# Summing the channel gate during the attention instead of ahead of the MLP

## The chip, the cores and the metric

The kernel runs on one core of a Trainium2 chip. The metric is the device time of one execution in microseconds (us). Every time and trace quoted here is of that one core. TensorE is called PE (PEld is its weight load), VectorE DVE, ScalarE ACT, GpSimd POOL and SyncE SP. SP issues all DMAs of this kernel.

## The reference

One layer of a streaming encoder on a sequence of 1024 tokens with 1024 channels, in float32:

```python
mod = silu(c) @ w_ada + b_ada                       # 6 rows of 1024
sh_a, sc_a, g_a, sh_m, sc_m, g_m = split(mod)
h = rmsnorm(x, g_attn_norm) * (1 + sc_a) + sh_a
proj = h @ w_in
o_mla = latent attention, 8 heads (low-rank q and kv, rotary part, chunk-causal)
o_ca  = chunked attention, 8 heads (9-chunk band, relative bias)
x = x + g_a * (concat(o_mla, o_ca) @ w_out)
h = rmsnorm(x, g_mlp_norm) * (1 + sc_m) + sh_m
u = causal depthwise convolution of width 3 over (h @ w_up)
gate, val = split(u)
x = x + g_m * ((silu(gate) * val) @ w_down)
```

`mod` has six rows of 1024 numbers, each a product of the vector silu(c) with a 1024x1024 block of `w_ada`. The change is about the last row, number 5, `g_m`: the gate of the channel sublayer. The other row that the text speaks of is number 2, `g_a`, and rows 3 and 4, shift and scale of the second norm.

## The kernel before

**Stages.** (1) Load `x`, norm it, compute rows 0 and 1, transpose `h` to channel layout and compute the first projection block. (2) The attention: 16 units of the chunked heads, then 16 units of the latent heads; a unit is 4 query tiles of one head. (3) Output projection of the latent heads, gated residual, second norm, transposes of the normed rows (`mod_transpose`, tile `ht_ps`). (4) The MLP: 44 column tiles of `w_up` (`up_tile`) and, in groups, `w_down` (`down`).

Matrix products are made in three products of split numbers (`gemm3`: high by high, high by low, low by high). So each weight tile is loaded raw, its high part is made by ACT (`hi_of`), its low part by POOL or DVE (`lo_of`).

**The attention and its fillers.** A query tile's steps are: scores on PE, softmax on DVE and ACT, a split into two half-precision parts (POOL, then DVE), a transpose by DMA (line 703, tile `PT`), and the product with V on PE (`pv`). Between these steps the code places other products, the fillers: the remaining projections (`qk1`, `qk2`, `v1`, `qk3`), the latent block (`m`), the up-projections of the latent heads (`up0`, `up1`) and the output projection of the chunked heads (`oca`). `pace` (called after every score and value step) runs fillers until an estimated PE cost is used up; `need` runs them until a named one is done. Each filler step says its own cost in ns of PE.

**The side work.** A generator `f_ada` (line 417) is advanced along the fillers. It makes rows 2, 3 and 4 in blocks of 256 columns: 8 loads of 128 KB of `w_ada` (`aw`, line 424) and a DVE multiply-add for each (`aacc`, lines 426 and 428), then a PE product that sums over partitions. For row 2 this is `gate_bcast` (line 449): it loads a piece of `b_ada` (`brow`), adds it, and multiplies with a matrix of ones, so that the sum stands on all 128 partitions; ACT copies it out (`gab`) and a DMA stores it to DRAM (`ga_d`). A block takes 6 steps of the generator. All these tiles come from `atile`, a pool of 3 buffers. `fill_step` (line 777) advances the generator by one step for each 2000 ns of filler cost, and not for `v0`, `up0`, `up1` and `oca`; what is left after the last filler is run at the end (`for _ in side[0]: pass`).

**Ahead of the MLP** (lines 892 to 908) row 5 is made in one piece: 8 loads of 512 KB into `adaw5`, summed by DVE (tile `adacc`, lines 902 and 904), `gate_bcast` twice with 512 columns (tile `p_gm`, line 454), and an ACT copy into `gmbc`. The `adaw5` tiles and the raw weight tiles of `up_tile` and `ff_tile` share one pool tag with 2 buffers:

```python
w = mp.tile([P, D], F32, name=f"adaw5_{k}", tag="raw", bufs=2)      # line 899
raw = mp.tile([P, ND, P], F32, name=f"wu_r{ch}", tag="raw", bufs=2) # line 911
```

`gmbc` is used when a raw tile of `w_down` is multiplied by it (line 938).

**What sets the order.** The order of instructions on each engine is fixed when the program is built: a list scheduler takes ready instructions by the order in the code, moved forward for the attention's steps (`high_priority`), on a model of the engines' times. Every engine, SP among them, then runs its list in order, and a tile is reused only after its last reader.

Of the kernel before, what the change touches and what calls it, by code (L numbers as in the profile page):

```python
# [12 lines left out]
F32 = mybir.dt.float32  # L13
# [4 lines left out]
AF = mybir.ActivationFunctionType  # L18
ALU = mybir.AluOpType
AX = mybir.AxisListType  # L20
PSUM = bass.MemoryType.PSUM
MUL, ADD, SUB, MIN, MAX = ALU.mult, ALU.add, ALU.subtract, ALU.min, ALU.max

P = 128
# [21 lines left out]

# columns of the packed constants
C_C, C_GA, C_GM, C_B, C_GQL, C_GKL = 0, 8, 16, 24, 72, 74
# [14 lines left out]
def layer_kernel(ctx, tc, I, out):  # L63
# [23 lines left out]
    part_d = dram.tile([NT, P, D], F32, name="part_d")  # L87
    ga_d = dram.tile([P, D], F32, name="ga_d")

    # ---------------- constants  # L90
    pk = cst.tile([P, NC_PACK], F32, name="pk")
# [23 lines left out]

    # =====================================================================
    # attention phase
    # =====================================================================
    right = tc.tile_pool(name="hw", bufs=1, side="right")
# [24 lines left out]
    def gemm3(pt, pairs, start=True, stop=True):  # L144
        """pairs: (stationary_hi, stationary_lo, moving_hi, moving_lo)"""
        n = len(pairs)
        for i, (sh, sl, mh, ml) in enumerate(pairs):
            pe.matmul(pt, sh, mh, start=(start and i == 0), stop=False)  # L148
            pe.matmul(pt, sh, ml, start=False, stop=False)  # L149
            pe.matmul(pt, sl, mh, start=False, stop=(stop and i == n - 1))  # L150

    # fillers: products that run between the steps of the attention, a few at a time,
    # queued behind the attention's latest products
    trail = []
# [11 lines left out]

    # ---- weights of one column block of the input projection, split once
    def load_w(name, src, ncol, he="a", ssw=None):
# [21 lines left out]

    # ---- x: statistics and normalised rows
    xs = []
# [20 lines left out]

    # ---- modulation rows and the first projection block, one slice of 128 channels at a time
    def mod_transpose(src, k, h, row, pspool, psum_tag, pb, hpool, tag, tmp, nbuf, veng, leng):
        """src(j): [128 tok, 128 ch] of 4 token tiles -> (hi, lo) of the modulated page [128, 2, 512]"""
        pt = pspool.tile([P, 512], F32, name=f"ht_ps{row}_{k}_{h}", tag=psum_tag, bufs=pb)
        for j in range(4):
            pe.transpose(pt[:, j * P:(j + 1) * P], src(j), ident[:])
        pg = hpool.tile([P, 2, 512], F32R, name=f"hT{row}_{k}_{h}", tag=tag, bufs=nbuf)  # L220
        a, b = modT[:, row, k:k + 1], modT[:, row + 1, k:k + 1]
        act.activation(pg[:, 0], pt[:], AF.Identity, scale=a, bias=b)
        v = tmp.tile([P, 512], F32, name=f"hv{row}_{k}_{h}", tag="hv", bufs=2)
        if veng == "a":
            act.activation(v[:], pt[:], AF.Identity, scale=a, bias=b)
        else:
            dve.tensor_scalar(v[:], pt[:], a, b, op0=MUL, op1=ADD)
        (dve if leng == "v" else pool).tensor_tensor(pg[:, 1], v[:], f32(pg[:, 0]), op=SUB)
        return pg
# [4 lines left out]
    for d in range(ND):  # L234
# [8 lines left out]
        for i in range(2):  # L243
            pe.matmul(pt[:, i:i + 1], acc[:, i, :], ones[:, 0:1], start=True, stop=True)
        # modT rows: 0 = gain of the norm * (1 + scale), 1 = shift
        tmp = cst.tile([P, 1], F32, name=f"adat{d}", tag="adat", bufs=2)
# [11 lines left out]

    # ---- rotary tables
    def rope_tables():  # L260
# [55 lines left out]
        act.activation(cn, cl2, AF.Sin)  # L316
        # per token: [g1 cos | g2 cos | g1 sin | g2 sin]
        for tab, c0 in ((tabq, C_RQ), (tabk, C_RK)):
# [11 lines left out]

    # ---- exact power-of-two scales that bring V into half precision's range, from a bound on |V|:
    # |sum_d x_d w_d|^2 <= n * sum_d b_d^2 w_d^2
    vscale = {}
# [25 lines left out]

    # ---- projection blocks  # L360
    def qk_norm(src_psum, nm, qn, j0):
        """[128, 2 tok tiles x 256] in PSUM -> normalised rows"""
        raw = rtile(f"raw{nm}")
        act.activation(raw[:], src_psum, AF.Copy)
        sq = qtile(f"sq{nm}")
        act.activation(sq[:], raw[:], AF.Square)
        ss = cst.tile([P, 8], F32, name=f"ss{nm}", tag="ss", bufs=4)
        r = cst.tile([P, 8], F32, name=f"r{nm}", tag="rr", bufs=4)
        dve.tensor_reduce(ss[:], sq[:].rearrange("p (a b) -> p a b", a=8), axis=AX.X, op=ADD)
        rsqrt_mean(r[:], ss[:], HD)  # L370
        pool.tensor_tensor(qn[:, j0:j0 + 2, :].rearrange("p t (a b) -> p (t a) b", a=4),
                           raw[:].rearrange("p (a b) -> p a b", a=8),
                           r[:].unsqueeze(2).to_broadcast([P, 8, HD]), op=MUL)
# [41 lines left out]

    # ---- the other adaLN rows
    def f_ada():
        for m in (2, 3, 4):
            for n in range(4):
# [13 lines left out]
                pt = ps.tile([P, 512], F32, name=f"p_ada{m}_{n}", tag="mm", bufs=2)  # L433
                if m == 2:
                    gate_bcast(pt[:, :256], acc, c0, 256, atile)
                    g = atile(f"gab{n}")
                    act.activation(g[:], pt[:, :256], AF.Copy)
                    sp.dma_start(ga_d[:, n * 256:(n + 1) * 256], g[:])
                else:
# [9 lines left out]
    def gate_bcast(pt, acc, c0, w, alloc):  # L449
        """column sums of acc, and b_ada, on every partition"""  # L450
        br = alloc(f"brow{c0}")
# [3 lines left out]

    # ---- latent block
    latT = {}

    def rope_apply(o, x, tab, t, nh, tmp):
        """o, x: [128, nh, 32]; tmp: [128, 2*nh*32]"""  # L460
        a = tmp[:, 0:nh * 32].rearrange("p (a b) -> p a b", a=nh)
# [41 lines left out]

    # ---- q_up / kv_up of 4 heads: token-layout q, k (normalised, rotated) and V stacks
    G = {}
# [76 lines left out]

    # ---- output projection of the chunked heads, kept aside in DRAM
    def load_wo(k0, n, he, le):
# [25 lines left out]

    # ---- attention
    def qk_page(src, name, rows, tag, bufs, gain):
        """src(j) -> [128 tok, rows] token-layout AP for the 4 token tiles of a half"""
        pt = ps.tile([P, 512], F32, name=f"{name}_ps", tag="T", bufs=TB)
# [11 lines left out]
    class Unit:  # L626
        """4 query tiles of one head"""

# [5 lines left out]
        def scores(u, i):  # L634
            """scores of one query tile and their softmax, transposed in two half-precision parts"""
            qpg, kpgs = u.pages()
# [140 lines left out]
    def fill_step():  # L777
        while fillers:
            key, gen = fillers[0]
            try:  # L780
# [4 lines left out]
                continue  # L785
            if key not in ("v0", "up0", "up1", "oca"):
                nside[0] += c
                while nside[0] > 2000:
                    nside[0] -= 2000
                    next(side[0], None)  # L790
# [39 lines left out]

    # =====================================================================
    # output projection of the latent heads, gated residual, second norm
    # =====================================================================
    wo = [load_wo(0, n, "a", "v" if n else "p") for n in range(2)]
# [48 lines left out]

    # =====================================================================
    # gated MLP with a causal depthwise convolution
    # =====================================================================
    mlp = tc.tile_pool(name="mlp", bufs=1, side="right", reuse_waits="tile")
# [3 lines left out]

    # gate of the channel sub-layer, on every partition
    def mtile(name):
        return mp.tile([P, D], F32, name=name, tag="u", bufs=3)

    gmbc = mp.tile([P, D], F32, name="gmbc")
    acc = mtile("adacc5")
    for k in range(ND):
        w = mp.tile([P, D], F32, name=f"adaw5_{k}", tag="raw", bufs=2)
        sp.dma_start(w[:], I["w_ada"][k * P:(k + 1) * P, 5 * D:6 * D])  # L900
        if k == 0:
            dve.tensor_scalar(acc[:], w[:], cs[:, 0:1], None, op0=MUL)
        else:
            dve.scalar_tensor_tensor(acc[:], w[:], cs[:, k:k + 1], acc[:], op0=MUL, op1=ADD)
    pt = ps3.tile([P, 1024], F32, name="p_gm", tag="U", bufs=2)
    for h in range(2):
        gate_bcast(pt[:, h * 512:(h + 1) * 512], acc[:, h * 512:(h + 1) * 512], 5 * D + h * 512, 512, mtile)
    act.activation(gmbc[:], pt[:], AF.Copy)

# [61 lines left out]
def _inputs(a):  # L971
    """layouts only: every array keeps its type and values"""
    f = lambda n: np.ascontiguousarray(a[n][0])
# [63 lines left out]
```

## Time and profile before

| what | us |
|---|---|
| median of 3 executions | 1525.28 (1518.91 to 1527.24) |
| span of the profiled execution | 1526.0 |
| PE busy | 1338.1 (88%) |
| DVE busy | 824.4 (54%) |
| POOL busy | 664.7 (44%) |
| ACT busy | 487.4 (32%) |
| latter part of the attention (400 to 680), PE busy | 215.3 of 280 |
| second norm's end to the first MLP product (770 to 795), PE busy | 4.2 of 25 |
| MLP (820 to 1500), PE busy | 675.0 of 680 |

For the profiled execution the trace gives its span, from the first to the last instruction of the program; no separate time of it is listed. The span is 0.7 us above the median of the runs. "Busy" is the time in which an engine executes an instruction. A row of instructions gives the line of the kernel, the engine, the operation, the tiles written and read, and the count; the bracket behind a row is how long the engine idled before it and what ended that. Times in windows are microseconds from the span's start.

### The profile page before, as it was taken

How to read it: one execution, taken by the hardware profiler on the slowest of the kernel's cores; microseconds unless marked ns; L12 is line 12 of the kernel's file. 1: busy time of each engine (PE TensorE's matmuls, PEld its weight loads, DVE VectorE, ACT ScalarE, POOL GpSimd, SP SyncE). 2: the span in 40 equal slices, each digit the busy share in tenths (PEclk: the TensorE clock that was granted, in tenths of full speed). 3: DMA queues.
4: the chain of work that ended last, by engine and by line, in shares of the span. 5: the costliest groups of instructions: out<-in, count | busy, mean ns of one | idle time of the engine just before them, and what ended most of it. 6: DMA issues, size and time to landing. Idle time of an engine off the chain costs nothing.

```text
span 1526.0 us, 19445 instructions
## 1 busy us (share of the span) xinstructions
PE 1338.1 (88%) x7100; PEld 1111.0 (73%) x7100; DVE 824.4 (54%) x1536; ACT 487.4 (32%) x919; POOL 664.7 (44%) x720
## 2 busy tenths in 40 slices
PE   3859989998767888858739999999999999999997
PEld 2749878987646666646528888888888888888885
DVE  6864786566768768843742433344334343434343
ACT  5443353343545545532413211212122121221200
POOL 5264463473799735435725231514314142341510
PEclk9979978989878899977859999999999999999998
DMA  7323657463613678787142110202112020110202
GB/s 270 133 67 73 138 119 142 121 131 94 122 40 70 150 143 174 165 181 247 56 138 69 56 55 28 70 30 67 42 42 69 15 83 28 56 56 28 70 1 110
DMA packets 202460, 142.90 MB, mean 94 GB/s; under 512 B 146294, under 2 KB 181242, under 8 KB 201340
## 3 DMA queue, kind: packets, MB, share of 16 engines
q1 hardware_dynamic: 202364, 141.66, 36.0%
q8 instruction: 56, 0.92, 0.3%
q14 instruction: 40, 0.33, 0.1%
HBM read 93.90 MB, written 13.11 MB: 70 GB/s over the span
## 4 chain that ended last, share of the span: by engine, by line
PE 63%; DMA 14%; DVE 10%; POOL 7%; issue 3%; ACT 2%; SPq 1%; POOLq 0%; DVEq 0%; ACTq 0%
PE up L148 10%; PE up L149 10%; PE up L150 10%; DMA aw<-w_ada 6%; PE dn L148 5%; PE dn L149 5%; PE dn L150 5%; DMA PTm<-hlm 4%; PE sc L656 2%; DVE adacc L241 2%; DVE aacc L428 1%; PE sm L656 1%; PE pvc L714 1%; POOL hlm L71 1%; DMA adaw<-w_ada 1%
## 5 line engine op out<-in xcount | busy, mean ns | idle before, releaser
L148 PE MATMUL up<-hT,wu_h 128*128 128x512 f32 x704 | 275.1, 391 | 0.0
L149 PE MATMUL up<-hT,wu_h 128*128 128x512 f32 x704 | 274.3, 390 | 0.0
L150 PE MATMUL up<-hT,wu_l 128*128 128x512 f32 x704 | 274.1, 389 | 0.0
L951 DVE TENSOR_TENSOR x<-x,dn 128x1024 f32<-128x1024 f32 x88 | 107.4, 1220 | 179.8 <-PE dn L150 179.8
L924 DVE SCALAR_TENSOR_TENSOR u<-up,pk,u 128x1023 f32<-128x1023 f32 x44 | 56.4, 1283 | 232.1 <-ACT u L923 232.1
L923 ACT ACTIVATE u<-up,pk 128x1024 f32<-128x1024 f32 x44 | 53.1, 1208 | 386.0 <-PE up L150 386.0
L149 PEld LDWEIGHTS up<-hT,wu_h 128*128 128x128 f32 x704 | 132.4, 188 | 28.0 <-issue 0.5
L148 PEld LDWEIGHTS up<-hT,wu_h 128*128 128x128 f32 x704 | 132.4, 188 | 27.9 <-issue 0.5
L82 POOL TENSOR_TENSOR wu_l<-wu_r,wu_h 128x1024 fp32r<-128x1024 f32 x44 | 105.7, 2402 | 107.9 <-PE up L149 60.1
L150 PEld LDWEIGHTS up<-hT,wu_l 128*128 128x128 f32 x704 | 132.4, 188 | 27.7 <-POOL wu_l L82 0.2
L77 POOL TENSOR_SCALAR wd<-wd_r 128x1024 fp32r<-128x1024 f32 x22 | 23.1, 1050 | 290.2 <-PE dn L150 289.1
L148 PE MATMUL dn<-wd,g 128*128 128x512 f32 x352 | 138.0, 392 | 5.0 <-ACT g L75 5.0
L149 PE MATMUL dn<-wd,g 128*128 128x512 f32 x352 | 137.9, 392 | 0.0
L150 PE MATMUL dn<-wd,g 128*128 128x512 f32 x352 | 137.4, 391 | 0.0
L71 POOL TENSOR_SCALAR hlm<-Pm,rim 128x512 f16<-128x512 f32 (+4 forms) x88 | 62.8, 717 | 69.1 <-DMA PTm<-hlm 46.6
L75 ACT ACTIVATE wu_h<-wu_r 128x1024 fp32r<-128x1024 f32 x44 | 46.5, 1057 | 141.1 <-DMA wu_r<-w_up 141.1
L938 POOL TENSOR_TENSOR wd_r<-wd_r,gmbc 128x1024 f32<-128x1024 f32 x22 | 52.6, 2392 | 80.6 <-DMA wd_r<-w_down 80.6
L701 DVE SCALAR_TENSOR_TENSOR hlm<-Pm,rim,hlm 128x512 f16<-128x512 f32 (+4 forms) x88 | 70.2, 801 | 31.7 <-POOL hlm L71 31.4
L148 PEld LDWEIGHTS dn<-wd,g 128*128 128x128 f32 x352 | 66.6, 189 | 19.4 <-issue 5.4
L71 POOL TENSOR_SCALAR hlc<-Pc,ric 128x640 f16<-128x640 f32 (+2 forms) x64 | 45.9, 719 | 78.5 <-DVE ric L684 38.9
L656 PE MATMUL sm<-mk,mq 96*128 96x512 f32 (+3 forms) x288 | 70.0, 375 | 9.8 <-ACT Pm L681 9.0
L656 PE MATMUL sc<-k,q 64*128 64x512 f32 (+3 forms) x288 | 71.2, 376 | 7.4 <-ACT Pc L681 4.9
(276 smaller groups left out, 3031.8 us busy)
## 6 DMA issues: line engine op xcount, KB each, us to landing
wu_r<-w_up SPq DMA_DIRECT2D x44, 512.0 KB, 3.6
aw<-w_ada SPq DMA_DIRECT2D x96, 128.0 KB, 2.2
wd_r<-w_down SPq DMA_DIRECT2D x22, 512.0 KB, 3.5
x<-x SPq DMA_DIRECT2D x16, 512.0 KB, 9.3
adaw<-w_ada_a SPq DMA_DIRECT2D x8, 1024.0 KB, 4.8
wq_r<-w_qk SPq DMA_DIRECT2D x32, 128.0 KB, 2.6
wor<-w_out SPq DMA_DIRECT2D x16, 256.0 KB, 3.0
cl<-oT_d SPq DMA_DIRECT2D x16, 256.0 KB, 3.3
```

What stands on the lines that cost most here:

```text
L71: pool.tensor_scalar(o, i, s, 1.0, op0=MUL, op1=MUL)
L75: act.activation(o, i, AF.Copy)
L82: (pool if eng == "p" else dve).tensor_tensor(o, i, f32(hi), op=SUB)
L148: pe.matmul(pt, sh, mh, start=(start and i == 0), stop=False)
L149: pe.matmul(pt, sh, ml, start=False, stop=False)
L150: pe.matmul(pt, sl, mh, start=False, stop=(stop and i == n - 1))
L656: last = pe.matmul(s[:, c:c + w], qpg[rs_, a, q], kpgs[kh][rs_, b, ko:ko + w], start=(a == 0 and b == 0), stop=(a == 1))
L701: dve.scalar_tensor_tensor(hl[:, w:2 * w], pp, ri[:], hl[:, :w], op0=MUL, op1=SUB)
L923: act.activation(u[:], pt[:], AF.Identity, scale=pk[:, cv + 2:cv + 3], bias=pk[:, cv + 3:cv + 4])
L924: dve.scalar_tensor_tensor(u[:, 1:], pt[:, :S - 1], pk[:, cv + 1:cv + 2], u[:, 1:], op0=MUL, op1=ADD)
L938: pool.tensor_tensor(raw[:], raw[:], gmbc[:], op=MUL)
L951: dve.tensor_tensor(x1[t][:], x1[t][:], pt[:], op=ADD)
```

## The change

Row 5 becomes part of `f_ada`: it is made in four blocks of 256 columns like row 2, and stored to a new DRAM tile `gm_d`. Ahead of the MLP, the 8 loads, the sums, the products and the copy are gone; one DMA loads `gmbc` from `gm_d`. In `fill_step` the generator is advanced along all fillers but `v0`, and by one step per 1800 ns of filler cost in place of 2000. (The change also takes out comments and docstrings, which shifts line numbers; those lines are left out here.)

```diff
     ga_d = dram.tile([P, D], F32, name="ga_d")
+    gm_d = dram.tile([P, D], F32, name="gm_d")
...
     def f_ada():
-        for m in (2, 3, 4):
+        for m in (2, 3, 4, 5):
             for n in range(4):
                 acc = atile(f"aacc{m}_{n}")
...
-                if m == 2:
+                if m in (2, 5):
                     gate_bcast(pt[:, :256], acc, c0, 256, atile)
                     g = atile(f"gab{n}")
                     act.activation(g[:], pt[:, :256], AF.Copy)
-                    sp.dma_start(ga_d[:, n * 256:(n + 1) * 256], g[:])
+                    sp.dma_start((ga_d if m == 2 else gm_d)[:, n * 256:(n + 1) * 256], g[:])
...
-            if key not in ("v0", "up0", "up1", "oca"):
+            if key != "v0":
                 nside[0] += c
-                while nside[0] > 2000:
-                    nside[0] -= 2000
+                while nside[0] > 1800:
+                    nside[0] -= 1800
                     next(side[0], None)
...
-    def mtile(name):
-        return mp.tile([P, D], F32, name=name, tag="u", bufs=3)
-
     gmbc = mp.tile([P, D], F32, name="gmbc")
-    acc = mtile("adacc5")
-    for k in range(ND):
-        w = mp.tile([P, D], F32, name=f"adaw5_{k}", tag="raw", bufs=2)
-        sp.dma_start(w[:], I["w_ada"][k * P:(k + 1) * P, 5 * D:6 * D])
-        if k == 0:
-            dve.tensor_scalar(acc[:], w[:], cs[:, 0:1], None, op0=MUL)
-        else:
-            dve.scalar_tensor_tensor(acc[:], w[:], cs[:, k:k + 1], acc[:], op0=MUL, op1=ADD)
-    pt = ps3.tile([P, 1024], F32, name="p_gm", tag="U", bufs=2)
-    for h in range(2):
-        gate_bcast(pt[:, h * 512:(h + 1) * 512], acc[:, h * 512:(h + 1) * 512], 5 * D + h * 512, 512, mtile)
-    act.activation(gmbc[:], pt[:], AF.Copy)
+    sp.dma_start(gmbc[:], gm_d[:])
```

## The prediction

> **What bounds the kernel now.** I read four views, in this order: busy time by stretches, the order of time around the end of the attention, the waits (of the engines, then of the DMA queue), and the rows of the loads that the change multiplies. The columns of the first are the stretch, its length, busy time and instruction count of PE, PEld, DVE, ACT and POOL, the granted clock, the DMA share and GB/s.
>
> ```profile
> 300.00:350.00 50.00, 47.64 (x294) 41.07 (x295) 34.31 (x104) 21.71 (x72) 35.79 (x62) 0.90 0.60 128
> 350.00:400.00 50.00, 42.15 (x250) 35.19 (x248) 32.13 (x87) 20.43 (x61) 23.06 (x49) 0.87 0.52 112
> 400.00:450.00 50.00, 32.09 (x151) 24.97 (x150) 35.18 (x93) 24.14 (x63) 45.96 (x87) 0.77 0.27 61
> 450.00:510.00 60.00, 48.69 (x278) 39.29 (x278) 49.71 (x131) 37.35 (x87) 57.10 (x100) 0.82 0.41 85
> 590.00:680.00 90.00, 68.22 (x501) 54.10 (x501) 65.02 (x158) 40.56 (x86) 40.49 (x50) 0.93 0.78 162
> 770.00:795.00 25.00, 4.21 (x6) 1.90 (x7) 11.76 (x11) 1.89 (x2) 2.63 (x2) 0.50 0.55 168
> 820.00:1500.00 680.00, 674.98 (x2974) 558.56 (x2974) 273.73 (x209) 135.24 (x125) 212.55 (x101) 1.00 0.15 47
> ```
>
> From 820 to 1500 PE is busy 675 of 680 us: the MLP is PE's own work, and whatever lets it start earlier ends the kernel earlier by as much. Directly before it PE works 4.2 us of 25. The attention has no such single limit: up to 400 PE nearly fills it (89.8 of 100 us), from 400 to 510 it is POOL (103 of 110), and after that no engine passes 76%.
>
> ```profile
> 766.09 1.97 PE L219 MATMUL ht_ps<-ident,xn 128*128 128x128 f32 x8 [0.93 <-DVE hv L227]
> 771.51 13.44 SPq L900 DMA_DIRECT2D adaw<-w_ada  x6
> 788.74 1.28 DVE L904 SCALAR_TENSOR_TENSOR adacc<-adaw,cs,adacc 128x1024 f32<-128x1024 f32 x1 [1.50 <-DMA adaw<-w_ada]
> 790.79 3.78 PE L454 MATMUL p_gm<-adacc,ones 128*128 128x512 f32 x4 [22.74 <-DVE adacc L453]
> 791.41 1.06 ACT L75 ACTIVATE wu_h<-wu_r 128x1024 fp32r<-128x1024 f32 x1 [22.55 <-DMA wu_r<-w_up]
> 793.59 1.42 PE L148 MATMUL up<-hT,wu_h 128*128 128x512 f32 x1
> 796.47 0.40 PE L150 MATMUL up<-hT,wu_l 128*128 128x512 f32 x1
> ```
>
> Here the hole is seen whole: the last transposes end at 768.06, the first `up` product starts at 793.59, 25.5 us later. Two waits hold it open together: `p_gm` stands ahead of `up` on PE, and the first `wu_r` could not be loaded, since its two `raw` buffers were taken by the eight `adaw` loads.
>
> ```profile
> SPq L424 <- DMA aw<-w_ada: 45.4, 34, 2.9
> SPq L438 <- ACT gab L437: 11.2, 2, 9.8
> PE pvm L714 <- DMA PTm<-hlm: 25.6, 21, 4.0
> L424 SPq DMA_DIRECT2D aw<-w_ada x96: 327/346/1147, 57.6 to 419.4; - x96
> L428 DVE SCALAR_TENSOR_TENSOR aacc<-aw,cs,aacc x84: 416/484/1544, 66.6 to 421.6; 128x256 f32<-128x256 f32 x84
> 294.19 0.49 POOL L113 TENSOR_SCALAR ss<-ss 128x8 f32<-128x8 f32 x1 [5.14 <-DVE ss L369]
> 286.01 0.20 POOL L113 TENSOR_SCALAR ss<-ss 128x8 f32<-128x8 f32 x1 [3.73 <-DVE ss L369]
> ```
>
> What the added work costs where such work already stands: SP holds 45.4 us for the slot of a load (waits by engine, count, longest), once 9.8 us for a `gab`; the values of the attention wait for transposes that go through the same SP. The loads end at 419; none stand in the latent heads.
>
> **The change, part by part.**
>
> *Removed, ahead of the MLP.* Eight 512 KB loads, eight DVE sums, two `brow`, four `p_gm` products and the copy into `gmbc`. What replaces the 25.5 us is the next thing that is late. The first `adaw` was issued at 746.29, when the last product of the output projection (745.8) freed the region. I take the same moment for what now comes first: `gmbc`, then `wu_r` twice, on SP. A 512 KB `adaw` landed after 4.4 us, so three behind one another land by about 746.3+3×4.4=759.5, the first `wu_r` by 755. ACT needs 1.06 us and POOL 2.36 us for it, in gaps that ACT shows at 1.3 and POOL at 1.6 us per pair of transposes: ready by about 761, before 768. The first 24 `up` products read pages of token half 0, done long before. So `up` can start at 768.06 or a little earlier between the transposes. Overshoot of POOL's gaps, 2.36−1.63=0.7 us for each of the first two tiles, delays the transposes by 0 to 1.5 us; `up` products slipped into PE's idle 5 us between 758 and 768 give back 0 to 2.3 us (ten products of 0.2275 us, the spacing at full clock). I set these against each other: 0.
>
> Clock: the stretch after the idle is granted 0.50, and `up` products take 0.63 us until 796.4, 0.39 after. Of that slow start of 5.6 us (790.8 to 796.4) `p_gm` now absorbs 2.8, `up` the rest. Without `p_gm` all of it falls on `up`: half of 2.8, 1.4 us more.
>
> So this part gains 25.5−1.4 = 24 us; bounds 19 (weights of the first tile ready only at 771.5 and a POOL delay) and 29 (a whole half tile, 24×0.2275=5.5 us, slipped in).
>
> *Added, in the attention.* Per block of 256 columns eight `aw` loads, a `brow`, a `gab` store; four blocks. SP: 32+4+4 issues at 0.346 us, 13.8 us. DVE: 28×0.484+4×0.354+4×0.406 = 16.6 us. PE: 4×0.377 = 1.5 us, ACT 4×0.381 = 1.5 us. Where: `f_ada` takes one step per 1800 of filler cost, from `qk1` on. The fillers `qk1`, `qk2`, `v1`, `qk3`, `m` sum to 120.2 us by their own formula, `up0` and `up1` to 13.0 each, `oca` to 41.4. Rows 2 to 4 have 72 steps, 130 us of filler; row 5 the next 24, up to 173 us. `m` ends at about 400 in the trace and `oca` runs from about 505 to 660, so row 5 stands between some 420 and 610, where the trace has none of these loads.
>
> Beside what: DVE has room (35 of 50, 50 of 60 us), SP too (at most 11.7 us of transposes in 20 us, 600 to 620). But the latent heads have no PE work in store, so delays show. Lower bound: nothing, since PE is idle 64 of the 280 us from 400 to 680 and the work fits the gaps. (Below nothing: a different order could also win a little; I know no reason that excludes some 3 us.) Upper bound: SP's queue in full. From the end of one DMA issue to the end of the next, a load took 1.36 us in the mean, a `gab` store 3.26, a `brow` 1.32: 32×1.36+4×3.26+4×1.32 = 62 us. Nearest row: 300 to 400 holds just 32 of these loads beside transposes, and PE is idle there 10.2 us (100−47.64−42.15) for any cause. Fillers covered part of the delays there, but not all of that idleness was the loads'. I take half, 5 us.
>
> POOL: its small `ss` takes 0.20 us, and 0.49 where it meets an `aacc`, 0.29 us more. With POOL the limit from 400 to 510, 28 such meetings would be 8 us, a third of them 2.7, which the 5 us include. [...]
>
> *Moved.* Rows 2 to 4 go at one step per 1800 in place of 2000: 66 steps in place of 60 by the end of `m`, in the part where PE is nearly full. The last two blocks, whose loads the trace already shows by 419 though the code has them at the end, get their products earlier than 662. Nothing waits for them before 736: 0. The reload of `gmbc` is counted above; its stores are done by 680.
>
> *Sum.* −24+5 = −19 us. The span is 1526.0; no time around it is given apart, and it stands 0.7 above the median of 1525.28. 1526.0−19 = 1507.0, against the median 1506.
>
> **The rivals.**
>
> *The added work costs nothing* and `up` slips in between the transposes: PE's 64 idle us and DVE's 30% speak for it, the values' 25.6 us of waiting for transposes against. 1525.3−24−0 to −29 = 1496 to 1501.
>
> *POOL or DVE pays in full.* Each `aacc` keeps POOL out for between the 0.29 us seen and its own 0.484: 28 of them 8 to 13.6 us, in 400 to 510; or DVE's 16.6 us stand in the path serially: 1525.3−24+8 to 16.6 = 1509 to 1518. For it: POOL 103 of 110. Against: row 5 reaches to 610, where POOL has half its time free.
>
> *SP blocks (slower).* SP runs in order; a load that waits for its buffer, or a `gab` store that waits for its product, holds back the transposes behind it, and PE waits for those. All 62 us on the path would end at 1563. It turns the sign at 24 of 62 us, 0.6 us per added issue on the path; slower by 0.5% needs 32, half of the queue time. For it: the 9.8 us `gab` wait, and DMA is 14% of the chain. Against: PE waited for the DMA of transposes 5.9 us in all from 300 to 400, with 32 loads there.
>
> *The hole does not close*: the weights' buffers come free late, or `gmbc` is late, so that little is won: 1518 to 1526. Against: their region is that of `adaw` and the freed output weights.
>
> **How the numbers follow.** Forecast (cost 2 to 8 us): 0.53. Nothing paid: 0.17. POOL or DVE: 0.14. SP blocks: 0.09. Hole stays: 0.07. The time is the first one's, 1506, with its own range 1502 to 1511. Down to 1496 and up to 1519 leaves out SP, the hole and some of the free case's tail: 0.2. About 0.5% (7.6 us) is what a measurement here tells from no change. Faster: 0.53+0.17+0.13=0.83; same: 0.01 of POOL's and the hole, 0.08; slower: 0.09.
>
> **What would show it.** After: no `p_gm` wait; `up` starting within 3 us of the last transpose; `wu_r` issued near 746 on the old clock; `aw` loads up to 500 or 600 with SP waits L424 grown by less than 25 us; the last transposes of the second norm at most 8 us later than 768. Wrong: that end moved by 20 us or more, or PE waiting for `PTm` 25 us longer.

## The result and the profile after

The changed kernel takes 1529.55 us in the median of 12 runs (1526.94 to 1534.07); the kernel before took 1522.96 on the same chip (12 runs, 1518.42 to 1527.64). The ratio is 1.0053, with an interval of 1.0036 to 1.0069: the change makes the kernel about 0.5% slower. 1506 was forecast, and the measured time lies outside the range of 1496 to 1519. The profiled execution took 1529.33 us, with a span of 1527.5. The kernel before was traced in one of its longer executions (its span, 1526.0, is 3.0 us above the median of its 12 runs, while in all other traces of this text the span is 1.8 to 2.4 us below the execution's time), so its times in the trace are late by up to some 5 us against its median, an estimate from these figures.

The order of time around the start of the MLP, in the kernel after (start, length, engine, line, operation, tiles, count; the bracket is the idle time before and what ended it):

```profile
751.94 0.49 SPq L894 DMA_DIRECT2D gmbc<-gm_d  x1
752.48 20.78 SPq L898 DMA_DIRECT2D wu_r<-w_up  x2
788.25 1.97 PE L220 MATMUL ht_ps<-ident,xn 128*128 128x128 f32 x8 [0.93 <-DVE hv L228]
790.94 1.99 ACT L75 ACTIVATE wu_h<-wu_r 128x1024 fp32r<-128x1024 f32 x2
792.04 0.80 PE L149 MATMUL up<-hT,wu_h 128*128 128x512 f32 x1 [1.81 <-ACT wu_h L75]
795.27 0.80 PE L151 MATMUL up<-hT,wu_l 128*128 128x512 f32 x1 [1.07 <-POOL wu_l L82]
```

The hole is closed as the prediction said. The weights are asked for from 752 on (the second tile some 20 us later), no `p_gm` is there, and the first `up` product starts 1.8 us after the last transpose. But this transpose ends at 790.2 instead of 768.1. The first `up` product starts at 792.0, where before it started at 793.6: of 23.7 us taken out of the hole, 22.1 had been lost by then. (By the medians, which differ by 6.6 us, it is more: 6.6+23.7, less 2.8 us by which the MLP got longer, leaves 27.5 us, in keeping with the long execution that was traced before.)

Where they were lost is seen in the stretches of the kernel after (length, then busy time and count of PE, PEld, DVE, ACT and POOL, granted clock, DMA share, GB/s):

```profile
350.00:400.00 50.00, 45.66 (x241) 38.85 (x240) 29.83 (x86) 18.29 (x58) 20.32 (x46) 0.80 0.47 101
400.00:450.00 50.00, 36.28 (x171) 28.87 (x170) 38.38 (x102) 27.80 (x69) 42.07 (x80) 0.75 0.33 77
450.00:510.00 60.00, 41.81 (x237) 33.98 (x238) 49.47 (x120) 32.65 (x77) 56.75 (x99) 0.81 0.38 84
590.00:680.00 90.00, 74.80 (x502) 59.96 (x501) 67.62 (x166) 42.79 (x90) 39.33 (x48) 0.89 0.76 160
770.00:795.00 25.00, 12.33 (x44) 7.99 (x44) 18.67 (x21) 12.19 (x18) 16.92 (x14) 0.57 0.07 21
820.00:1500.00 680.00, 674.99 (x2979) 558.71 (x2977) 273.91 (x210) 135.45 (x126) 214.96 (x102) 1.00 0.15 47
```

The MLP is PE's own work as before. From 450 to 510 PE makes 237 products where it made 278; from 350 to 400 it makes 241 in 45.7 us where it made 250 in 42.2, at a clock of 0.80 instead of 0.87. The attention is behind by then and stays so: the chunked heads end 7.7 us later than before and the latent heads 23.5. Its busiest engines are the same, and no new one is full.

The waits of the whole span, of SP's queue and of PE, in the kernel after (waiter, what it waited for, us in all, times, longest). Line 439 is the store of a `gab`; its wait is put down to the ACT instruction that came last.

```profile
SPq L425 <- DMA aw<-w_ada: 38.5, 30, 4.0
SPq L439 <- ACT kraw L568: 12.6, 1, 12.6
PE pvm L715 <- DMA PTm<-hlm: 22.6, 14, 3.3
PE sm L657 <- ACT Pm L682: 18.6, 16, 6.4
```

The last of them in the kernel before:

```profile
PE sm L656 <- ACT Pm L681: 9.0, 11, 2.2
```

The loads in the kernel after:

```profile
L425 SPq DMA_DIRECT2D aw<-w_ada x128: 323/376/1570, 55.9 to 616.4; - x128
```

The 32 further loads stand up to 616, as forecast. SP's wait for their buffers did not grow (45.4 before, 38.5 now), nor did PE's wait for the transposed values (25.6 before, 22.6 now). A single new block of SP is seen: from 466 to 478.7 the store of a `gab` holds it for 12.6 us. One wait of PE did grow, that of the latent heads' scores (`sm`) for ACT, from 9.0 to 18.6; no rival had named it, and it does not explain the time by itself (in the kernels below it is 8.3 in the fast `e5`, but 7.1 in the slow `k2`). So none of the marks that the rivals named is large, and yet 22 us are gone. A trace of the whole change can't tell which part took them; the runs below take it apart.

### The profile page after: what moved, and what is told of

Same layout as the page of the kernel before. It is cut to its first block, busy times and chain, and to the rows that moved or that the text cites. A ratio compares the mean times of both kernels' runs of the same rounds, so it can differ in the third digit from the quotient of the medians.

```text
span 1527.5 us, 19553 instructions
## 1 busy us (share of the span) xinstructions
PE 1353.6 (89%) x7104; PEld 1125.6 (74%) x7104; DVE 832.3 (54%) x1562; ACT 489.2 (32%) x922; POOL 660.1 (43%) x720
## 4 chain that ended last, share of the span: by engine, by line
PE 54%; POOL 5%; DVE 4%; DMA 4%; issue 2%; ACT 2%; SPq 0%; POOLq 0%; ACTq 0%; DVEq 0%
PE up L151 11%; PE up L149 10%; PE up L150 10%; PE dn L149 5%; PE dn L150 5%; PE dn L151 5%; DMA PTm<-hlm 2%; PE sm L657 2%; PE pvm L715 1%; DVE hlm L702 1%; DMA cl<-oT_d 1%; DVE mm L676 1%; POOL hlm L71 1%; PE op L151 1%; POOL x L871 1%
## 5 line engine op out<-in xcount | busy, mean ns | idle before, releaser
L657 PE MATMUL sm<-mk,mq 96*128 96x512 f32 (+3 forms) x288 | 74.5, 393 | 19.1 <-ACT Pm L682 18.6
L429 DVE SCALAR_TENSOR_TENSOR aacc<-aw,cs,aacc 128x256 f32<-128x256 f32 x112 | 62.7, 560 | 43.8 <-DMA aw<-w_ada 42.9
```

Source lines behind the costliest of these rows:

```text
L657: last = pe.matmul(s[:, c:c + w], qpg[rs_, a, q], kpgs[kh][rs_, b, ko:ko + w], start=(a == 0 and b == 0), stop=(a == 1))
```

## The experiments

All ratios are against the kernel before on the same chip, with 95% intervals. In us, 0.1% is 1.5. The median of the kernel before lies between 1522 and 1524.6 from chip to chip, so ratios are compared, not medians. The milestones are from the profiled execution of each kernel.

### Row 5 and the pace, each alone

`e1`: the change, but with the pace of before. `e2`: the kernel before with the new pace only. `e3`: the change without row 5's work (row 5 is left out, and `gmbc` is loaded from row 2's store instead; so too in all kernels below that are said to be without row 5). `e5`: the kernel before without row 5's work.

```diff
 e1, in fill_step of the kernel after
-            if key != "v0":
+            if key not in ("v0", "up0", "up1", "oca"):
-                while nside[0] > 1800:        # and the line below
+                while nside[0] > 2000:
 e2, in fill_step of the kernel before: the reverse
 e3, in the kernel after
-        for m in (2, 3, 4, 5):
+        for m in (2, 3, 4):
-    sp.dma_start(gmbc[:], gm_d[:])
+    sp.dma_start(gmbc[:], ga_d[:])
 e5: e3 with e1's lines
```

> The changed kernel with the old pace: one step of the side work per 2000 ns of filler cost, and none along v0, up0, up1 and oca, so that row 5 stands at the end of the side work. Theory A (row 5's own loads, sums and stores cost the 22 us that the attention lost): the attention still loses them, 1520 to 1530 us. Theory B (the new pace, that is the new order of the instructions, costs them, whatever row 5 does): the attention ends as before and the hole is closed, 1499 to 1504. Both by halves: about 1512.

> The kernel before with nothing but the new pace (one step per 1800 ns, along all fillers but the first); row 5 is still made ahead of the MLP. Theory A: no change, 1521 to 1525 us. Theory B: the attention's 22 us are lost and the hole stays, 1543 to 1547. By halves: about 1533, since the scores of the chunked heads were already 7 to 10 us late in the changed kernel before the first load of row 5.

> The changed kernel without row 5: the side work makes rows 2 to 4 at the new pace, and the gate of the channel sublayer is loaded from row 2's store instead (row 5 is left out of the computation). Theory A: the hole is closed at no cost, 1499 to 1502 us. Theory B: the attention still ends 22 us late, 1521 to 1525. By halves: about 1511.

> The attention's side work as before (rows 2 to 4, one step per 2000 ns, not along v0, up0, up1, oca), row 5 left out of the computation (row 2's store is loaded in its place). It prices the hole alone. If the new pace cost the changed kernel 10 us and row 5's work 12 us, the attention ends here as before (first output-projection product at 685 to 688 us) and the time is 1524 less 24 to 28, 1496 to 1500. If any change in the code behind the attention moves the attention too, it ends some 10 us off, 1506 to 1510.

| kernel | median us | ratio | last value product, chunked heads | same, latent heads | last transpose | first `up` | span |
|---|---|---|---|---|---|---|---|
| before | 1522.96 | 1 | 411.6 | 681.3 | 768.1 | 793.6 | 1526.0 |
| after | 1529.55 | 1.0053 [1.0036, 1.0069] | 419.3 | 704.8 | 790.2 | 792.0 | 1527.5 |
| `e1` | 1549.64 | 1.0166 [1.0146, 1.0186] | 413.4 | 681.0 | 811.2 | 813.0 | 1548.4 |
| `e2` | 1541.49 | 1.0113 [1.0094, 1.0132] | 416.6 | 692.7 | 783.0 | 808.0 | 1539.3 |
| `e3` | 1522.20 | 0.9982 [0.9969, 0.9995] | 417.9 | 690.4 | 781.2 | 783.0 | 1517.8 |
| `e5` | 1502.12 | 0.9858 [0.9833, 0.9884] | 409.2 | 677.9 | 764.5 | 766.3 | 1501.9 |

The three parts come out of the table. Taking row 5 out and leaving all else gives −1.42%, 21.6 us: that is the hole (`e5`). The new pace costs 1.24%, 18.9 us, with no row 5 anywhere (`e3` against `e5`), and 1.13%, 17 us, with row 5 still ahead of the MLP and the hole still open (`e2`). Row 5's own work in the attention costs 0.71%, 10.8 us (after against `e3`; the two medians differ by 7.4). −21.6+18.9+10.8 = 8.1 us, the measured 0.53%; they add up by construction, since `e5` and `e3` are steps on the way from before to after.

`e1` shows why the pace was changed together with the rest. Without it row 5's steps are not used up by the fillers, and what is left is made in one piece behind the last of them, where PE has nothing else to do. PE's waits from 670 to 745 in `e1`:

```profile
PE p_ada L455 <- DVE aacc L454: 54.4, 4, 16.5
```

The hole was only moved there from the start of the MLP, and grew.

### The rate, or the fillers that count

The new pace has two halves: 1800 in place of 2000, and `up0`, `up1` and `oca` counted. `e6` and `e7` take one half each, without row 5; `g2` is the whole change but for the rate.

```diff
 in fill_step of e3
 e6: if key not in ("v0", "up0", "up1", "oca"):   with 1800
 e7: if key != "v0":                              with 2000
 g2: the kernel after                             with 2000
```

> As the run without row 5, with one step per 1800 ns but still not along up0, up1 and oca. If the denser steps in the chunked heads cost the 10 us: 1506 to 1510. If the steps along the latent heads' fillers cost them: 1496 to 1500. If it is each new order's own luck: anywhere between 1490 and 1520, with no sum of the two halves.

> As the run without row 5, with one step per 2000 ns, along all fillers but the first. If the denser steps cost the 10 us: 1496 to 1500. If the steps along the latent heads' fillers cost them: 1506 to 1510; the last two blocks of rows 2 to 4 are then the only work that has moved. If it is each order's own luck: anywhere between 1490 and 1520.

> The whole change, but with one step per 2000 ns as before, along all fillers but the first; row 5 in the attention. If the rate of 1800 cost 11 us there as it did without row 5 (1522.2 against 1511.1) and row 5's own work 7 us: 1516 to 1521, faster than the kernel before. If row 5's work costs more once the steps stand further apart and run to the end of the attention: 1525 to 1535.

| without row 5 | old fillers | all but `v0` |
|---|---|---|
| 2000 | `e5` 0.9858 [0.9833, 0.9884] | `e7` 0.9913 [0.9888, 0.9937] |
| 1800 | `e6` 1.0005 [0.9988, 1.0021] | `e3` 0.9982 [0.9969, 0.9995] |

`g2` took 1516.81 us, 0.9949 [0.9933, 0.9966]. So the rate is the larger half: 1.47% with the old fillers, 0.69% with all. Counting more fillers costs 0.55% at 2000 and costs nothing at 1800 (−0.23%). The halves don't add. Row 5's work costs 0.36% at 2000 (`g2` against `e7`), 5.5 us. With the rate left at 2000 the change would have made the kernel faster by 0.5%.

### Is it the density of the side work?

My theory then was that a step per 1800 is too dense: more loads and sums in the same stretch, with PE nearly full. It expects the time to fall steadily as the steps stand further apart. The rival: each rate is another order of all instructions, and the order decides. Four more rates, with the old fillers and no row 5, differ from `e6` in the number alone.

> The run without row 5 along the old fillers, with one step per 1900 ns: between 2000 (1502.1 us) and 1800 (1524.6 us). If denser steps cost by themselves, it lies between them, 1508 to 1518. Theory E, that each order meets or misses single stalls by chance: it may as well be at 1500 or at 1530.

> The run without row 5 along the old fillers, with one step per 2200 ns; 2000 gave 1502.1 us, 1900 1525.5, 1800 1524.6. If thinner steps are better by themselves: 1495 to 1502. If the rate of 2000 is a lucky order among many: 1510 to 1530.

> The run without row 5 along the old fillers, with one step per 2100 ns. So far the last value product of the attention ended at 677.9 us with 2000, 681.8 with 2200, 697.4 with 1900 and 693.5 with 1800. Theory F (steps denser than one per 2000 ns of filler cost cost 16 to 20 us, thinner ones nothing): that end at 677 to 683. Theory E (chance): anywhere from 672 to 700.

> The same with one step per 1950 ns, the smallest change from 2000. Theory F in its smooth form: the end of the last value product between that of 2000 and 1900, at 680 to 692 us. Theory E: anywhere from 672 to 700; an end beyond that of 1900 (697) or before that of 2000 (678) speaks for chance.

| ns per step | median us | ratio | last value product, latent heads | DVE's multiply-adds wait for loads, 100 to 700 |
|---|---|---|---|---|
| 1800 (`e6`) | 1524.56 | 1.0005 [0.9988, 1.0021] | 693.5 | 37.9 |
| 1900 (`g3`) | 1525.53 | 1.0023 [1.0005, 1.0041] | 697.4 | 41.7 |
| 1950 (`m2`) | 1519.12 | 0.9980 [0.9966, 0.9995] | 689.9 | 48.8 |
| 2000 (`e5`) | 1502.12 | 0.9858 [0.9833, 0.9884] | 677.9 | 41.2 |
| 2100 (`m1`) | 1522.98 | 0.9999 [0.9983, 1.0015] | 690.5 | 52.9 |
| 2200 (`g4`) | 1517.35 | 0.9967 [0.9953, 0.9981] | 681.8 | 46.0 |

The theory falls. 2000 is the fastest, with a slower kernel on both sides of it; 1900 is no faster than 1800, 1950 still loses most of it, and 2100 is as slow as 1800. At 2100 and 2200 a known wait is part of it: their last block is left over, and PE waits 11.6 and 11.0 us for its sums ahead of the output projection. Without it 2200 would stand near 1506, an estimate, so 2200 alone would not speak against the theory. But at 2100 the latent heads, too, end 12.6 us later than at 2000. The kernels that lose do so in different places. Those with 1800 that I followed (after, `e3`, `e6`) fall back between 178 and 193: PE idles 4.4, 4.1 and 4.0 us there, at a mean granted clock of 0.78, 0.89 and 0.77, where `e5` idles 1.4 us at 1.00. By these figures it is some 4 to 5 us of PE's work, an estimate. 1950 loses there too (4.4 us idle, 0.89); 1900 does not (1.3 us, 1.00), and falls back between 400 and 420 instead, where PE is busy 11.4 of 20 us and in `e5` 15.4.

How one such loss comes about can be seen in the trace. DVE in the kernel after, then PE:

```profile
184.92 0.49 DVE L429 SCALAR_TENSOR_TENSOR aacc<-aw,cs,aacc 128x256 f32<-128x256 f32 x1
185.44 0.75 DVE L624 SCALAR_TENSOR_TENSOR k<-k_ps,gk_ca,k 128x512 fp32r<-128x512 f32 x1
```

```profile
186.24 1.22 PE L657 MATMUL sc<-k,q 64*128 64x128 f32 x4 [3.81 <-DVE k L624]
```

The same two in the kernel before:

```profile
184.45 0.75 DVE L623 SCALAR_TENSOR_TENSOR k<-k_ps,gk_ca,k 128x512 fp32r<-128x512 f32 x1
```

```profile
185.25 0.72 PE L656 MATMUL sc<-k,q 64*128 64x128 f32 x4 [0.31 <-DVE k L623]
```

DVE runs its list in order, and waits for loads in it (of `aw`, 1.4 to 2.1 us each around here). In the kernel after, one sum more and an `oc` (the result of a value product) stand ahead of the split of `k` that PE's next scores need: `k` comes 1 us later. That alone would be little. But in the kernel before, PE had a value product and fillers ready for these 4 us, and in the kernel after it has almost none there. The stretches of after (columns as above), and then that of before:

```profile
182.00:186.00 4.00, 0.44 (x2) 0.24 (x2) 2.29 (x4) 0.00 (x0) 0.00 (x0) 1.00 0.22 66
186.00:189.00 3.00, 2.76 (x11) 2.53 (x12) 1.88 (x11) 1.02 (x4) 0.37 (x1) 0.54 0.21 44
189.00:192.00 3.00, 3.00 (x16) 3.00 (x15) 1.14 (x4) 1.23 (x2) 0.48 (x1) 0.50 0.15 30
192.00:196.00 4.00, 4.00 (x21) 2.87 (x20) 2.07 (x8) 0.67 (x2) 1.84 (x2) 0.87 0.25 60
```

```profile
182.00:186.00 4.00, 3.01 (x26) 2.54 (x25) 1.63 (x3) 0.69 (x2) 0.71 (x1) 1.00 0.40 104
```

The gap of 3.81 us is paid more than once: until about 193 PE then works at half the clock (0.54 and 0.50 from 186 to 192), so that it makes 27 products in 6 us. PE's busy time over the span grew from 1338.1 to 1353.6 us, with 7104 products in place of 7100; this place makes up some 3.4 us of it, an estimate (half of the time at half the clock), and the rest was not followed. In the kernel before, with its wait of 0.31 us, the granted clock is 1.00 from 182 to 196. After the gap of 3.81 us it took some 6.8 us to come back, from 186.24 to 193.0, worked out from the 0.87 of the last stretch. It is not always so long. In `e3` PE idles 3.50 us at the same place, and the stretch behind it is:

```profile
186.00:192.00 6.00, 6.00 (x33) 5.31 (x32) 3.23 (x12) 2.24 (x6) 1.54 (x4) 0.72 0.17 34
```

A mean of 0.72 over 6 us is 3.4 us at half the clock. In `e6`, with a gap of 3.45 us, the same stretch has 0.50, so it is 6 us or more there. The length of the gap alone does not decide it.

### The loads, or the sums

Since the pace moves loads (SP, DMA) and sums (DVE) alike, `h1` takes the loads away from `e6` (all sums read one resident tile) and `h2` the time of the sums (one column each). `i1` is the kernel after with one load for the eight sums of a row-5 block.

```diff
 h1, in f_ada of e6 (and atile's pool with 2 buffers, to make room for awc)
-                    w = atile(f"aw{m}_{n}_{k}")
-                    sp.dma_start(w[:], I["w_ada"][k * P:(k + 1) * P, c0:c0 + 256])
+                    w = awc
 h2, in place of the two sums of e6
+                    dve.tensor_scalar(acc[:, k:k + 1], w[:, 0:1], cs[:, k:k + 1], None, op0=MUL)   # and one memset of acc per block
 i1, around the load of the kernel after
+                    if m < 5 or k == 0:
```

> The 1800 run without row 5 and along the old fillers (1524.6 us, against 1502.1 at 2000), but all sums of the side work read one resident tile in place of 96 loaded ones (so rows 2 to 4 come out as other numbers; one of the side work's three buffers is given up for it). Theory C (at 1800 the sums stand in DVE's fixed order too early, wait there for their loads, and hold back the attention's own DVE work behind them): with nothing to wait for the loss goes, 1498 to 1508 us. Theory D (the sums' own DVE time, 51 us, is what costs): nothing goes, 1518 to 1525. Theory E (any new order of the instructions falls by chance): anywhere.

> The same 1800 run with the 96 loads, but each sum cut to one column, so that DVE waits for the load and then works next to nothing (rows 2 to 4 come out as other numbers). Theory C: the waits stay and most of the loss with them, 1515 to 1525 us. Theory D: the loss goes, 1495 to 1505. Theory E: anywhere.

> The changed kernel with one load in place of eight for each block of row 5, its eight sums all reading that tile (row 5 comes out as other numbers). If row 5's loads and their waits are what its 7 us in the attention are made of: 1521 to 1525 us, as without row 5 (1522.2). If its sums, products and stores are: 1527 to 1531, as the changed kernel (1529.6).

`h1` took 1496.91 us, 0.9819 [0.9802, 0.9836]; `h2` 1512.66, 0.9932 [0.9918, 0.9945]; `i1` 1522.82, 1.0004 [0.9993, 1.0016]. Without loads the rate of 1800 is faster than any kernel with loads: 28 us against `e6`, more than the pace costs. PE's wait for transposed values of the chunked heads between 140 and 420, first in `e6`, then in `h1`:

```profile
PE pvc L715 <- DMA PTc<-hlc: 9.2, 8, 2.9
```

```profile
PE pvc L717 <- DMA PTc<-hlc: 1.6, 3, 0.7
```

The chunked heads end at 390.2 in `h1` and at 416.1 in `e6`, so nearly all of it is won there. (The wait is 9.1 us in `e5` too: it is a price of the loads at either rate, not of 1800.) With the loads and nearly no sums, 11 us are won. In row 5's part, 28 of the 32 loads make 0.49% (after against `i1`), 7.5 us, most of row 5's 10.8. It is a mixed difference: from the end of the chunked heads to that of the latent heads `i1` needs 271.2 us and the kernel after 285.5, but its chunked heads end at 425.3, 6.0 us later than those of the kernel after, although in the kernel after all but two of row 5's loads stand behind that point. So the loads, waited for in queues that run in order, look like the larger part of what makes the side work dear, and the DVE time of the sums like the smaller. These runs change the order too, so each price has the scatter of the table of rates on it; and no kernel without loads was run at 2000, so how much of `h1`'s 28 us belongs to the rate of 1800 is not shown.

### Can the waiting be taken off DVE?

If a sum that waits for its load holds up what is behind it on DVE, loads issued a step earlier than their sums should help. `k1` is the kernel after with the two loads of a step issued ahead and their sums queued one step later, behind the latest split of the softmax (line 702); `k2` has the same sums in `v1`, the kernel told of next.

```diff
+                for k0 in range(0, ND, 2):
+                    ws = [load(k0), load(k0 + 1)]      # as before, two loads
+                    yield 0
+                    with (tc.issue_after(dtrail[-1]) if dtrail else ExitStack()):
+                        ...                            # their two sums
```

> The changed kernel, complete, with one thing more: the sums of a pair of loads are emitted one step later than the loads and queued on DVE behind the last split (line 702) that the attention has emitted by then. Theory C (sums that reach DVE's queue before their load has landed hold back the attention): DVE waits for the loads much less than the changed kernel's 43 us, and a large part of the 20 us lost in the attention comes back, 1505 to 1517 us. Theory E (any order loses by chance): waits fall but the time need not, 1510 to 1535.

> The best kernel so far (row 5 in the MLP with own buffers, the attention's side work as before, 1505.4 us) with the same late sums for rows 2 to 4. Theory C: part of the 41 us for which DVE waits for loads there goes, 1495 to 1503 us. Theory E: as likely slower as faster, 1497 to 1520.

DVE's wait for the loads from 100 to 700, in the kernel after and in `k1`:

```profile
DVE aacc L429 <- DMA aw<-w_ada: 40.7, 40, 2.8
```

```profile
DVE aacc L436 <- DMA aw<-w_ada: 33.3, 35, 3.8
```

The wait fell as meant (in `k2` to 25.7, from 38.9 in `v1`), and both became slower: `k1` 1541.85 us, 1.0117 [1.0094, 1.014], `k2` 1538.51, 1.0103 [1.009, 1.0117]. But this is no clean test of the idea. In `k2` the last sums, tied to the latest split, come only after the attention (the last load of `aw` at 721.0, in `v1` at 419.5), and PE waits for them ahead of the output projection, which it does not in `v1`. PE's wait from 680 to 800 in `k2`:

```profile
PE p_ada L445 <- DVE aacc L435: 25.3, 2, 16.5
```

These 25.3 us are most of the 33 us by which `k2` is slower than `v1`. In `k1` a load now holds SP once for 19.7 us and once for 12.1, waiting for its buffer in the latent heads; the longest such wait in the kernel after is 4.0:

```profile
SPq L428 <- DVE modT L451: 19.7, 1, 19.7
```

The chunked heads do end earlier with late sums, 9.9 us in `k1` and 5.1 in `k2`, and the loss lies behind them: from there to the end of the latent heads `k1` needs 305.8 us instead of 285.5, and `k2` 290.4 instead of 272.8. So these two runs show that late sums in this form don't pay, but not that DVE's waiting for loads costs nothing; that SP's new waits are the cause is not shown. In the table of rates, with the same work, the sum of DVE's waits does not rank the times: `e5`, the fastest, has more of it than `e6`. Where a wait falls seems to count for more than how much of it there is.

### Row 5 where PE covers it

The hole can also be closed with the attention left alone. `e4` and `v1` are the kernel before with row 5 behind the first two `up` tiles, so that PE has work while the row is loaded and summed. In `e4` the loads keep the two `raw` buffers that the weights use; in `v1` they and the sum stand in buffers of the MLP that are not needed yet (`g` and `wd`). Both put `p_gm` into PSUM tiles of `down`.

```diff
     def ff_tile(j):
         ug = up_tile(j)
         uv = up_tile(NF + j)
+        if j == 0:
+            gate_row()                       # the old block, as a function
 in gate_row, v1 against e4
-            w = mp.tile([P, D], F32, name=f"adaw5_{k}", tag="raw", bufs=2)
+        ws = [mp.tile([P, 2, S], F32, name=f"adaw5_{k}", tag="g", bufs=4) for k in range(2)]
+            w = ws[k // 2 % 2][:, k % 2]
```

> The kernel before, with row 5 made in one piece behind the first two column tiles of w_up instead of ahead of them, its products in the PSUM buffers of the down-projection; nothing in the attention is touched. Both theories: the attention ends as before, the hole at 770 closes, and row 5's sums lie beside PE's own work: before less 23 us, 1498 to 1502. If the hole has another cause than the loads and the place of the products of row 5, it stays at 1521 to 1525.

> Row 5 made in the MLP as in the run before with that place, but its loads and sums in buffers of the later g and wd tiles, so that the raw weight tiles wait for nothing. If that run's 25 us of PE idleness inside the MLP came from the raw buffers, they go: 1498 to 1503 us. If they came from the place of the gate's products in PE's order, ahead of weights that are ready, PE still waits for them, less long since four loads fly together: 1505 to 1515.

`e4` took 1534.55 us, 1.0066 [1.0043, 1.0088]. Its hole is closed (the first `up` at 765.9), but PE idles 29.9 us in the MLP where the kernel before has 5.0. PE's waits from 764 to 860, and SP's queue:

```profile
PE p_gm L454 <- DVE adacc L453: 18.7, 1, 18.7
```

```profile
769.14 37.10 SPq L898 DMA_DIRECT2D adaw<-w_ada  x8
```

The eight loads pass through the two `raw` buffers at the pace of DVE's sums, and no weights come in for those 37 us: the hole was moved again. With buffers of its own (`v1`) row 5 is loaded beside the weights, and PE idles 6.1 us in the MLP:

```profile
766.76 1.97 PE L219 MATMUL ht_ps<-ident,xn 128*128 128x128 f32 x8 [0.93 <-DVE hv L227]
770.54 0.79 PE L148 MATMUL up<-hT,wu_h 128*128 128x512 f32 x1 [1.81 <-ACT wu_h L75]
```

`v1` takes 1505.42 us (1501.77 to 1508.68), 0.9873 [0.985, 0.9896], with the whole computation. It beats both kernels, and stands 0.15%, 2.3 us, above `e5`, which has no row 5 at all; the intervals of the two overlap. Its attention ends as before (last transpose at 768.7).

## Why the prediction was wrong, step by step

**What bounds the kernel: right.** The MLP is PE's own work, and the 25.5 us ahead of it were open idle time. **Removed, −24: right.** `e5` gives 21.6 us and `v1` 19.3, both within the bounds of 19 to 29. The size was short by the two terms that I had set against each other: `up` did not start in the gaps of the transposes but 1.8 us after the last, since ACT makes `wu_h` only at 790.94, behind its last copy of the transposes, though the first weights had been asked for at 752.5. The time from the first `up` to the last `down` product grew by 2.8 us (727.5 to 730.3): PE's busy time in it by 1.8, where the clock had been taken as 1.4, and its idle time by 1.1, nearly all of it the wait for `wu_l` at 795.27. So 25.5−1.8−2.8 = 20.9 is what closing the hole was worth. The base was less sure than it looked, too: the forecast stood on a median of three runs, 1525.28, and on that of twelve, 1522.96, the same sum gives 1504.

**Added, 5: low by up to a half.** Row 5's work costs 5.5 us at a rate of 2000 and 7.4 to 10.8 at 1800, inside the bounds (0 to 62). PE's part was put at half its size (a block of row 2 has two records of 0.377 us, so 3.0 us and not 1.5), but the sum did not use it. Its reason was partly right: the loads seem to make most of it (`i1`), by waiting in queues. The largest single block was SP's 12.6 us at a `gab` store, the rival's mechanism, but PE's waits for transposes did not grow.

**Moved, 0: wrong, and this decided it.** "Nothing waits for them before 736: 0" looked only for a reader of rows 2 to 4 that would get them late. The cost was not in who reads them but in who stands behind them: the pace sets where each load and sum is placed in the lists of SP and DVE, and through the scheduler the order on all engines. It cost 17 to 19 us, almost all of the gain (`e2`, `e3` against `e5`). For a different order the prediction had only some 3 us of gain, in the bounds of the step before. I gave this step no bounds, though the trace of before doesn't show the new order; a step that the trace doesn't show had to have them from both sides.

**The rivals and the signs.** SP as the blocker was the only slower one, and it isn't what decided: SP's waits for load buffers fell and PE's for `PTm` too, and the pace costs as much with row 5's added issues left out. The rival on POOL took each of 28 sums to hold POOL up by 0.29 to 0.484 us, an estimate from single rows. The trace of before shows it for some instructions only: `ss` (128x8) took 0.24, 0.49 and 0.44 us where the sum of a load (`aacc`) ran beside it, and ended 0.05 to 0.06 us after that sum, against a median of 0.20 in the other 13; the split `hlc` (128x640) took 0.80 in the median both beside one (11) and without (21). POOL's busy time from 400 to 510 was 103.1 us before and 98.8 after. The signs of the hole came as written (no `p_gm`, `up` within 3 us, loads to 616, SP's waits not grown), but for `wu_r`, which was asked for 37.7 us ahead of the last transpose and not 22, and so did the sign for wrong: the last transpose moved by 22 us.

**What stays open.** Shown is that the pace takes the 17 to 19 us, that the rate is most of it, and that the time does not follow the density. A kernel at 1800 without the loads is 28 us faster than one with them, but without its like at 2000 that doesn't show the loads to be the reason. Why the order at 2000 fits so well, 17 to 23 us better than 1800, 1900, 1950 and 2100, is not settled: one loss (at 182 to 193) is followed to its wait, but it accounts for some 4 to 5 us, and other rates lose elsewhere. Whether deeper load buffers would take the scatter away was not tried.

## What to carry to other kernels

A constant that says how fast side work is fed into a scheduled program is not a volume control: each value is another order of every engine's list, and here neighbouring values lie up to 23 us apart, 1.5%, with the same work. So a "moved" step has a price with bounds on both sides, and they are as wide as this scatter; before a loss is explained by too much or too little of something, a few neighbouring values should be run.

Idle time ahead of a stage that fills one engine was closed best here by putting the missing work inside that stage, under that engine, with buffers that its own loads don't need (`v1`, −1.3%). The same move with shared buffers (`e4`, +0.7%), or into a stage bound by waits (the change, +0.5%, and −0.5% at the old rate), moved the hole or paid for it elsewhere.

## What the runs showed of the hardware

A wait of PE was paid more than once where nothing covered it: after 3.81 us of idling in the kernel after, PE worked for about 6.8 us at half the clock (granted 0.54, then 0.50), so some 3.4 us more were lost (an estimate, half of the 6.8). After 3.50 us of idling in `e3` it was 3.4 us at half the clock (a mean of 0.72 over 6 us), so some 1.7 more. And the time that DVE spent waiting for loads said little by itself here: with the same work, 37.9 us of it stand beside 1524.56 us (`e6`) and 41.2 beside 1502.12 (`e5`).
